# Summing one tile's gathered expert rows by matmuls, and two streams that share six PSUM banks

## The chip, the cores and the metric

One core of a Trainium2 chip runs the kernel. Its engines work in parallel, each through its own queue of instructions in a fixed order: PE (TensorE, matmuls into PSUM), DVE (VectorE), ACT (ScalarE), POOL (GpSimd, which here issues the gathers) and SP (SyncE, which issues all other DMAs). They wait for one another by semaphores. PSUM has eight banks of 128 x 512 fp32. The metric is device microseconds of one execution.

## The reference

One layer of a decoder for 1024 prompt tokens and 8 sample tokens, with d = 1024. The trunk is a combined projection `h @ w_in`, three mixers (dilated attention, gMLP, a linear recurrence) and `w_out`. Behind it comes PEER: each token picks, per head, 16 of 16384 single-neuron experts, 8 x 16 = 128 in all.

```python
x = x + g1 * (mix @ w_out)
h2 = rmsnorm(x, norm_ffn) * (1 + sc2) + sh2
q = rmsnorm((h2 @ w_q).reshape(n, 8, 2, 128))
s = einsum('nhpe,hpke->nhpk', q, sub_keys)        # top 16 of each half, then top 16 of the pairs
act = gelu(einsum('nd,nkd->nk', h2, u_tab[e]))    # 128 rows of u per token
out = einsum('nk,nkd->nd', softmax_gate * act, v_tab[e])   # and 128 rows of v
x = x + g2 * out
```

## The kernel before

The prompt is eight tiles of 128 tokens (0 to 7); tile `NT` = 8 holds the sample tokens. The program has two halves.

The trunk is written group by group (`GROUPS`): `project` (stream Z) makes q, k, v and the mixers B and C of a group's tiles from five blocks of `w_in`; `mix_and_route` (stream R) does attention, `w_out`, the query product with `wq` and the top-16 of the keys; `select` finishes the choice of experts. Each stream takes its PSUM banks from tags of its own: Z two for products (`za`) and one for the rest (`zs`), R two and two, and the gate table of the dense tiles one (`g`), eight in all. `sample_attention` stands behind group 1.

PEER is computed in two ways. Tiles 1, 3, 4 and 5 (`DENSE`) go through all 16384 experts by matmuls (`dense`): 128 chunks of u and v are loaded, split into two fp32r parts, multiplied into `psS`, gated (`a`<-`a`,`gc`) and multiplied into `psK` and `psO`; it starts when the trunk's PSUM and SBUF pools are closed (`fctx.close()`), with `xr` loads from DRAM. Tiles 0, 2, 6 and 7 (`GATHER`) and the sample go through gathered rows (`experts`): for each of the 128 choices k, one indirect DMA of POOL fetches into a `grow` buffer (five of them) the row of choice k for each of the 128 tokens, a token on each partition. A u row is reduced against x by DVE into `dot`; a v row is scaled by DVE and added to `acc` (L933). Each gather moves 128 x 4 KB, 0.524 MB.

The order on each engine is made by a scheduler from the order of the program text: what is written earlier goes first when it is ready. In the text the gathered tiles come last, but their gathers need only POOL, DVE and DMA, so they are taken up as soon as a tile's experts are chosen.

Of the kernel before, what the change touches and what calls it, by code (L numbers as in the profile page):

```python
# [10 lines left out]
F32 = mybir.dt.float32  # L11
F32R = mybir.dt.float32r
BF = mybir.dt.bfloat16
I32 = mybir.dt.int32
U32 = mybir.dt.uint32
AF = mybir.ActivationFunctionType
ALU = mybir.AluOpType
# [4 lines left out]
D = 1024  # L22
NT = 8
GATHER = (0, 2, 6, 7)
DENSE = (1, 3, 4, 5)
PROJECT = ((0, 1, NT), (), (2, 3), (4, 5), (6, 7))
GROUPS = ((0,), (1,), (2, 3, NT), (4, 5), (6, 7))
ND = len(DENSE)
GRP = 4
TB = 16  # L30
OHB = 4
BANKS = dict(za=2, zs=1, ra=2, rs=2, g=1)
GST = 8
LK = 2
SJ = 4
RES = 4
RAW = 6
# [9 lines left out]
P = 128  # L47
# [13 lines left out]
def kernel(ctx: ExitStack, tc: tile.TileContext, I, O):  # L61
    nc = tc.nc
    V, A, G, T, S = nc.vector, nc.scalar, nc.gpsimd, nc.tensor, nc.sync

    dpool = ctx.enter_context(tc.tile_pool(name="dpool", bufs=1, space=DRAM))
    gat = ctx.enter_context(tc.tile_pool(name="gat", bufs=2))
    se = ctx.enter_context(tc.tile_pool(name="se", bufs=1))
    fctx = ExitStack()
    mm = fctx.enter_context(tc.tile_pool(name="mm", bufs=1, space=PSUM))
# [4 lines left out]
    class Stream:  # L74
# [3 lines left out]
            self.key, self.rows = key, rows  # L78

        def ps(self, name="ps", kind="s"):  # L80
            return mm.tile([P, 512], F32, tag="p" + self.key + kind, name=name, bufs=BANKS[self.key + kind])

        def load_w(self, src):
            ws = []
# [16 lines left out]
    R = Stream("r", 4)  # L101

    class Early:

        n = 0
# [18 lines left out]
    ident = fc.tile([P, P], F32, name="ident")  # L124
# [641 lines left out]
            y = rstd(R, qss[t], P, 16, 1.0 / P)  # L766
            V.tensor_tensor(tv[t][0], tv[t][0], y[:, :, None].to_broadcast([P, 16, 16]), op=ALU.mult)

    tr = {}

    def select(t):
        if t == NT:

            tv[t] = (se.tile([P, 16, 16], F32, tag="tkv", name="tkv", bufs=3), se.tile([P, 16, 16], U32, tag="tki", name="tki", bufs=3))
            v1, x1 = (q[:, 0, :] for q in tv[t])
            sr = R.a2("sr")[:, :P]
            S.dma_start(sr, s_d.rearrange("b (s k) -> (b s) k", k=P))
            top16(sr, P, v1, x1, "tkw", P)
            S.dma_start(sv_d, v1)
            S.dma_start(sx_d, x1)  # L780
            v, x = (q[:64, 2:4, :] for q in tv[t])
            S.dma_start(v, sv_d.rearrange("(q two) k -> q two k", two=2))
            S.dma_start(x, sx_d.rearrange("(q two) k -> q two k", two=2))
            r, nh = 64, 1
        else:
            r, nh = P, 8
            v, x = tv[t]
        tv.pop(t)
        i1, i2, gt = (se.tile([P, 8, 16], F32, tag=nm, name=nm, bufs=1)[:r, :nh] for nm in ("d_i1", "d_i2", "d_g"))
        yield from select_experts(v, x, r, nh, i1, i2, gt)  # L790
        if t in h2_d:
            e = se.tile([P, 8, 16], I32, tag="d_q4", name="d_e", bufs=1)[:r, :nh]
            V.scalar_tensor_tensor(e, i1, float(P), i2, op0=ALU.mult, op1=ALU.add)
            for d, src in ((e_d[t], e), (w_d[t], gt)):
                S.dma_start(dram_ap(d, 0, [[16 * nh, r], [1, 16 * nh]]), src.rearrange("p h k -> p (h k)"))
            return
        ps = R.ps("psi")
        tr[t] = fr.tile([P, 3, P], F32, tag="tr", name="tr", bufs=2)
        for q, src in enumerate((i1, i2, gt)):
            T.transpose(ps[:, q * P:(q + 1) * P], src.rearrange("p h k -> p (h k)"), ident)  # L800
        A.copy(tr[t], ps[:, :3 * P].rearrange("p (q n) -> p q n", q=3))

    def gate_ps(name):
        return mm.tile([P, 512], F32, tag="pg", name=name, bufs=BANKS["g"])

    def gate_table(t):

# [106 lines left out]
    def gather_rows(tab, idx):  # L914
        rt = grow("grow")
        G.indirect_dma_start(out=rt, out_offset=None, in_=tab, in_offset=bass.IndirectOffsetOnAxis(ap=idx, axis=0))  # L916
        return rt

    def experts(x, eidx, gate, n):

        w = gat.tile([P, n], F32, tag=f"dot{n}", name="dot", bufs=1)
        for k in range(n):
            rt = gather_rows(I["peer_u"], eidx[:, k:k + 1])
            V.scalar_tensor_tensor(rt, rt, 1.0, x, op0=ALU.mult, op1=ALU.mult, accum_out=w[:, k:k + 1])  # L924
        A.activation(w, w, AF.Gelu_apprx_tanh)
        V.tensor_tensor(w, w, gate, op=ALU.mult)
        acc = gat.tile([P, D], F32, tag="gx", name="acc", bufs=1)
        for k in range(n):
            rt = gather_rows(I["peer_v"], eidx[:, k:k + 1])
            if k == 0:  # L930
                V.tensor_scalar(acc, rt, w[:, 0:1], None, op0=ALU.mult)
            else:
                V.scalar_tensor_tensor(acc, rt, w[:, k:k + 1], acc, op0=ALU.mult, op1=ALU.add)  # L933
        return acc

    def finish(t, peer, alloc):
        g2 = gate_row("g2", t, alloc)
# [13 lines left out]
    def peer_prompt(t):  # L951
        e, w, x = routed(t, [P, P], lambda d: d)
        S.dma_start(x, h2_d[t])
        acc = experts(x, e, w, P)
        finish(t, acc, grow)

    def peer_sample():
# [124 lines left out]
    def now(gen):  # L1082
        for _ in gen:
            pass
# [20 lines left out]
    for t in GROUPS[-1]:  # L1105
        if t in DENSE:
            now(select(t))
            now(gate_table(t))
    fctx.close()
    dense()  # L1110
    for t in GROUPS[-1]:
        if t not in DENSE:
            now(select(t))
    for t in GATHER:
        peer_prompt(t)
    peer_sample()

def _t5_bucket(dist):
# [85 lines left out]
```

## Time and profile before

| | us |
|---|---|
| median of three runs (lowest, highest) | 3285.99 (3276.42, 3286.62) |
| the profiled execution | 3281.25 |
| its span, from the first to the last instruction | 3279.5 |
| busy: PE, DVE, ACT, POOL | 2791.1, 2537.5, 1224.6, 1409.8 |

967.86 MB are moved, 295 GB/s over the span; 545.33 MB of them by POOL's queue. The chain of work that ended last is spread over PE (26% of the span), DMA (22%), the time to issue (21%), POOL (16%) and DVE (10%), so no engine bounds the whole, and the halves are to be read apart. PE's time for an fp32 matmul is written in two records, so 704 products of `psz` stand as 1408.

### The profile page before, as it was taken

To read this page: it belongs to the slowest core of one execution; us is meant where nothing else is said; L and a number is where in the kernel's file an instruction comes from. 1 tells how busy PE (TensorE), PEld (TensorE's weight loads), DVE (VectorE), ACT (ScalarE), POOL (GpSimd) and SP (SyncE) were. 2 spreads that over 40 slices of the span, in tenths; PEclk is the share of its full clock that TensorE was granted. 3 is DMA by queue.
4 is the path that set the end of the run, shared out by engine and by line. 5 is a ranking of instruction groups with operands and counts; after the bars stand their busy time and mean duration, and the time that the engine had idled before them with its cause. 6 is when DMAs were issued, how large, how long until landed. Compare 5 with 4: busy or idle time off the path is not lost.

```text
span 3279.5 us, 36013 instructions
## 1 busy us (share of the span) xinstructions
PE 2791.1 (85%) x11152; PEld 1883.0 (57%) x11152; DVE 2537.5 (77%) x5342; ACT 1224.6 (37%) x2725; POOL 1409.8 (43%) x1046
## 2 busy tenths in 40 slices
PE   6889788789888899777598999888989999889895
PEld 2334334544355445545287777777777777678774
DVE  1434776778877798777999898788888978888986
ACT  3443434755366545656342222221322222222220
POOL 0000323454223431334226655566556556666663
PEclk8889987889999999878799999999999999999997
DMA  7567888897867985788869998899999989999997
GB/s 250 178 210 255 323 270 262 263 352 258 300 211 268 339 279 186 259 281 280 297 235 332 335 342 325 324 326 350 337 330 342 334 308 343 342 344 344 323 337 230
DMA packets 347343, 967.86 MB, mean 295 GB/s; under 512 B 36335, under 2 KB 120870, under 8 KB 345102
## 3 DMA queue, kind: packets, MB, share of 16 engines
q0 software_dynamic: 149760, 545.33, 47.0%
q1 hardware_dynamic: 197390, 420.23, 36.7%
q8 instruction: 88, 1.44, 0.2%
q14 instruction: 105, 0.86, 0.1%
HBM read 909.28 MB, written 60.88 MB: 296 GB/s over the span
## 4 chain that ended last, share of the span: by engine, by line
PE 26%; DMA 22%; issue 21%; POOL 16%; DVE 10%; ACT 4%; SPq 0%; POOLq 0%; DVEq 0%; ACTq 0%
POOL grow L916 16%; PE psz L249 10%; DMA grow<-in_peer_v,ge 8%; DMA g_d<-st 3%; PE psG L823 3%; DMA grow<-in_peer_u,ge 3%; DMA w<-in_wq 2%; DVE acc L933 2%; PE psO L1038 2%; PE pst L174 2%; PE pso L637 2%; PE lg L620 1%; PE psa L206 1%; PE psS L1022 1%; DVE grow L924 1%
## 5 line engine op out<-in xcount | busy, mean ns | idle before, releaser
L916 POOL DMA_INDIRECT grow<-in_peer_u,ge x520 | 698.6, 1343 | 1189.6 <-DVE grow L924 526.1
L916 POOL DMA_INDIRECT grow<-in_peer_v,ge x520 | 710.6, 1366 | 658.5 <-DVE acc L933 365.9
L249 PE MATMUL psz<-w,hT 128*128 128x512 f32 x1408 | 699.2, 629 | 66.8 <-DMA w<-in_wq 33.8
L933 DVE SCALAR_TENSOR_TENSOR acc<-grow,dot,acc 128x1024 f32<-128x1024 f32 x515 | 660.0, 1282 | 117.8 <-DMA grow<-in_peer_v,ge 111.3
L924 DVE SCALAR_TENSOR_TENSOR grow<-grow,gx 128x1024 f32<-128x1024 f32 x520 | 626.1, 1220 | 137.9 <-DMA grow<-in_peer_u,ge 114.0
L249 PEld LDWEIGHTS psz<-w,hT 128*128 128x128 f32 x1408 | 258.5, 201 | 324.9 <-issue 225.4
L1038 PE MATMUL psO<-vh,ah 128*128 128x512 f32 x512 | 225.8, 441 | 138.9 <-DVE acc L1047 138.5
L991 ACT CAST vh<-v 128x1024 fp32r<-128x1024 f32 x128 | 125.2, 1047 | 494.2 <-PE psO L1038 492.3
L823 PEld LDWEIGHTS psG<-o,oh 128*128 128x128 f32 x1024 | 163.9, 221 | 169.3 <-ACT st L825 106.2
L823 PE MATMUL psG<-o,oh 128*128 128x128 f32 x1024 | 197.2, 325 | 69.6 <-ACT st L825 64.0
L991 ACT CAST ah<-a 128x512 fp32r<-128x512 f32 x128 | 79.6, 622 | 435.6 <-DVE a L1027 435.6
L815 DVE TENSOR_TENSOR oh<-iof,tr 128x1024 f32<-128x1024 f32 x128 | 156.4, 1224 | 105.5 <-PE psG L823 104.2
L1038 PE MATMUL psO<-vl,ah 128*128 128x512 f32 x512 | 219.5, 429 | 0.0
L991 ACT CAST uh<-u 128x1024 fp32r<-128x1024 f32 x128 | 134.9, 1054 | 224.5 <-PE psS L1022 224.4
L1038 PE MATMUL psO<-vh,al 128*128 128x512 f32 x512 | 217.9, 426 | 0.0
L1038 PEld LDWEIGHTS psO<-vh,ah 128*128 128x128 f32 x512 | 109.2, 213 | 176.5 <-DVE acc L1047 151.9
L822 ACT ACTIVATE o<-oh,tr 128x128 f32<-128x128 f32 x512 | 185.2, 400 | 55.2 <-PE psG L823 47.9
L1038 PE MATMUL psK<-vh,ah 128*128 128x512 f32 x512 | 201.0, 393 | 4.2 <-ACT ah L991 4.2
L1038 PE MATMUL psK<-vh,al 128*128 128x512 f32 x512 | 200.7, 392 | 0.3 <-DVE al L992 0.3
L1038 PE MATMUL psK<-vl,ah 128*128 128x512 f32 x512 | 200.5, 392 | 0.0
L992 DVE TENSOR_TENSOR ul<-u,uh 128x1024 fp32r<-128x1024 f32 x128 | 156.2, 1220 | 2.8 <-ACT uh L991 2.7
L992 DVE TENSOR_TENSOR vl<-v,vh 128x1024 fp32r<-128x1024 f32 x128 | 150.7, 1220 | 1.3 <-ACT vh L991 1.0
(372 smaller groups left out, 5029.1 us busy)
## 6 DMA issues: line engine op xcount, KB each, us to landing
u<-in_peer_uT SPq DMA_DIRECT2D x128, 512.0 KB
v<-in_peer_v SPq DMA_DIRECT2D x128, 512.0 KB
w<-in_w_in SPq DMA_DIRECT2D x80, 512.0 KB
w<-in_wq SPq DMA_DIRECT2D x80, 512.0 KB
g_d<-st SPq DMA_DIRECT2D x64, 512.0 KB
gc<-g_d SPq DMA_DIRECT2D x16, 2048.0 KB
w<-in_w_ada SPq DMA_DIRECT2D x48, 512.0 KB
w<-in_w_out SPq DMA_DIRECT2D x40, 512.0 KB
```

The source lines that it names most:

```text
L174: T.transpose(pv[:, c, :r], src[:, (c0 + c) * P:(c0 + c + 1) * P], ident[:r, :r])
L249: T.matmul(ps, xT[:, c, :], w(c), start=(c == 0), stop=(c == 7))
L637: T.matmul(po[64 * hh:64 * hh + 64, :P], vt[:, c, 64 * hh:64 * hh + 64], pT[c // 4][:, c % 4, :], start=(c == 0), stop=(c == t))
L815: V.tensor_tensor(oh, iof[:, None, None, :].to_broadcast([P, 2, OHB, P]), tt[:, 0:2, b * TB + n0:b * TB + n0 + OHB, None].to_broadcast([P, ...
L822: A.activation(o1, oh[:, 0, n0 % OHB + q, :], AF.Copy, scale=tt[:, 2, n:n + 1])
L823: T.matmul(ps[:, q * P:(q + 1) * P], oh[:, 1, n0 % OHB + q, :], o1, start=True, stop=True)
L916: G.indirect_dma_start(out=rt, out_offset=None, in_=tab, in_offset=bass.IndirectOffsetOnAxis(ap=idx, axis=0))
L924: V.scalar_tensor_tensor(rt, rt, 1.0, x, op0=ALU.mult, op1=ALU.mult, accum_out=w[:, k:k + 1])
L933: V.scalar_tensor_tensor(acc, rt, w[:, k:k + 1], acc, op0=ALU.mult, op1=ALU.add)
L991: A.copy(hi, x)
L992: eng.tensor_tensor(lo, x, hi, op=ALU.subtract)
L1038: T.matmul(ps, aa[x][:, t * P:(t + 1) * P], vv[y][:, hf * 512:(hf + 1) * 512], start=(k == 0 and (first or o not in keep)), stop=(k == 3 * ...
```

## The change

Tile 0's v rows are gathered by token: for a token, its 128 chosen rows, one on each partition. The indices for that are `eT`, the transpose of the tile's choices, made in `select`. The sum over the 128 choices is then a contraction over partitions, one matmul per half row: its stationary operand is a block `wz` of 32 columns that is zero but for the column of the token, which holds the token's 128 weights from `wT`, so the products of 32 tokens add up in the 32 partitions of their column group. Two PSUM banks (`pacc`) hold the sum of the tile. They are two of the eight; the other six become the tags `a` and `s` of three banks each, for both streams and the gate table. `wz` takes a buffer of R's `a2`. Tile 0's PEER is written in front of `fctx.close()`. `LK`, the buffers of the lookup, goes from 2 to 1.

```diff
--- before.py
+++ after.py
@@ -22,6 +22,7 @@
 D = 1024
 NT = 8
 GATHER = (0, 2, 6, 7)
+ROWS_PE = (0,)
 DENSE = (1, 3, 4, 5)
 PROJECT = ((0, 1, NT), (), (2, 3), (4, 5), (6, 7))
 GROUPS = ((0,), (1,), (2, 3, NT), (4, 5), (6, 7))
@@ -29,9 +30,9 @@
 GRP = 4
 TB = 16
 OHB = 4
-BANKS = dict(za=2, zs=1, ra=2, rs=2, g=1)
+BANKS = dict(a=3, s=3)
 GST = 8
-LK = 2
+LK = 1
 SJ = 4
 RES = 4
 RAW = 6
@@ -78,7 +79,7 @@
             self.key, self.rows = key, rows
 
         def ps(self, name="ps", kind="s"):
-            return mm.tile([P, 512], F32, tag="p" + self.key + kind, name=name, bufs=BANKS[self.key + kind])
+            return mm.tile([P, 512], F32, tag="p" + kind, name=name, bufs=BANKS[kind])
 
         def load_w(self, src):
             ws = []
@@ -766,7 +767,7 @@
             y = rstd(R, qss[t], P, 16, 1.0 / P)
             V.tensor_tensor(tv[t][0], tv[t][0], y[:, :, None].to_broadcast([P, 16, 16]), op=ALU.mult)
 
-    tr = {}
+    tr, eT = {}, {}
 
     def select(t):
         if t == NT:
@@ -791,6 +792,13 @@
         if t in h2_d:
             e = se.tile([P, 8, 16], I32, tag="d_q4", name="d_e", bufs=1)[:r, :nh]
             V.scalar_tensor_tensor(e, i1, float(P), i2, op0=ALU.mult, op1=ALU.add)
+            if t in ROWS_PE:
+                ef = se.tile([P, 8, 16], F32, tag="d_t", name="d_ef", bufs=1)
+                V.scalar_tensor_tensor(ef, i1, float(P), i2, op0=ALU.mult, op1=ALU.add)
+                ps = R.ps("pse")
+                T.transpose(ps[:, :P], ef.rearrange("p h k -> p (h k)"), ident)
+                eT[t] = gat.tile([P, P], I32, tag="eT", name="eT", bufs=1)
+                V.tensor_copy(eT[t], ps[:, :P])
             for d, src in ((e_d[t], e), (w_d[t], gt)):
                 S.dma_start(dram_ap(d, 0, [[16 * nh, r], [1, 16 * nh]]), src.rearrange("p h k -> p (h k)"))
             return
@@ -801,7 +809,7 @@
         A.copy(tr[t], ps[:, :3 * P].rearrange("p (q n) -> p q n", q=3))
 
     def gate_ps(name):
-        return mm.tile([P, 512], F32, tag="pg", name=name, bufs=BANKS["g"])
+        return R.ps(name, "a")
 
     def gate_table(t):
 
@@ -916,7 +924,7 @@
         G.indirect_dma_start(out=rt, out_offset=None, in_=tab, in_offset=bass.IndirectOffsetOnAxis(ap=idx, axis=0))
         return rt
 
-    def experts(x, eidx, gate, n):
+    def weights(x, eidx, gate, n):
 
         w = gat.tile([P, n], F32, tag=f"dot{n}", name="dot", bufs=1)
         for k in range(n):
@@ -924,6 +932,11 @@
             V.scalar_tensor_tensor(rt, rt, 1.0, x, op0=ALU.mult, op1=ALU.mult, accum_out=w[:, k:k + 1])
         A.activation(w, w, AF.Gelu_apprx_tanh)
         V.tensor_tensor(w, w, gate, op=ALU.mult)
+        return w
+
+    def experts(x, eidx, gate, n):
+
+        w = weights(x, eidx, gate, n)
         acc = gat.tile([P, D], F32, tag="gx", name="acc", bufs=1)
         for k in range(n):
             rt = gather_rows(I["peer_v"], eidx[:, k:k + 1])
@@ -933,6 +946,32 @@
                 V.scalar_tensor_tensor(acc, rt, w[:, k:k + 1], acc, op0=ALU.mult, op1=ALU.add)
         return acc
 
+    def experts_by_rows(t, x, eidx, gate):
+
+
+        w = weights(x, eidx, gate, P)
+        ps = R.ps("pswT")
+        T.transpose(ps[:, :P], w, ident)
+        wT = gat.tile([P, P], F32, tag="wT", name="wT", bufs=1)
+        A.copy(wT, ps[:, :P])
+        acc = [mm.tile([P, 512], F32, tag=f"pacc{hf}", name="pacc", bufs=1) for hf in range(2)]
+        for m in range(32):
+            if m % 4 == 0:
+                wz = R.a2("wz").rearrange("p (m j c) -> p m j c", m=4, j=4)
+                V.memset(wz, 0.0)
+                for i in range(4):
+                    V.tensor_copy(wz[:, i, :, m + i], wT.rearrange("p (j m) -> p j m", j=4)[:, :, m + i])
+            for j0 in (0, 2):
+                rows = [(j, gather_rows(I["peer_v"], eT[t][:, 32 * j + m:32 * j + m + 1])) for j in (j0, j0 + 1)]
+                for hf in range(2):
+                    for j, row in rows:
+                        T.matmul(acc[hf][32 * j:32 * j + 32, :], wz[:, m % 4, j, :], row[:, hf * 512:(hf + 1) * 512],
+                                 start=(m == 0), stop=(m == 31))
+        out = gat.tile([P, D], F32, tag="gx", name="acc", bufs=1)
+        for hf in range(2):
+            A.copy(out[:, hf * 512:(hf + 1) * 512], acc[hf])
+        return out
+
     def finish(t, peer, alloc):
         g2 = gate_row("g2", t, alloc)
         x1 = alloc("x1f")
@@ -951,7 +990,7 @@
     def peer_prompt(t):
         e, w, x = routed(t, [P, P], lambda d: d)
         S.dma_start(x, h2_d[t])
-        acc = experts(x, e, w, P)
+        acc = experts_by_rows(t, x, e, w) if t in ROWS_PE else experts(x, e, w, P)
         finish(t, acc, grow)
 
     def peer_sample():
@@ -1106,13 +1145,16 @@
         if t in DENSE:
             now(select(t))
             now(gate_table(t))
+    for t in ROWS_PE:
+        peer_prompt(t)
     fctx.close()
     dense()
     for t in GROUPS[-1]:
         if t not in DENSE:
             now(select(t))
     for t in GATHER:
-        peer_prompt(t)
+        if t not in ROWS_PE:
+            peer_prompt(t)
     peer_sample()
 
 def _t5_bucket(dist):
```

PE around the end of the trunk. `pss` is the trunk's last product, `psS` the dense half's first. Before:

```order
L249 MATMUL psz<-w,hT 128x512 x5
L174 MATMUL pst<-ident,q 128x128 x4
L753 MATMUL pss<-keysT,q2T 128x128 x4
L1022 MATMUL psS<-x0h,uh 128x512
L1022 MATMUL psS<-x0l,uh 128x512
```

and now:

```order
L250 MATMUL psz<-w,hT 128x512 x5
L175 MATMUL pst<-ident,q 128x128 x4
L754 MATMUL pss<-keysT,q2T 128x128 x4
L954 MATMUL pswT<-ident,dot 128x128
L968 MATMUL pacc<-grow,wz 32x512 x256
L1061 MATMUL psS<-x0h,uh 128x512
L1061 MATMUL psS<-x0l,uh 128x512
```

All 256 matmuls on tile 0's v rows, and the transpose of their weights, have come to stand in one run between the two halves.

PE in the trunk, where group 1's attention (`lg_1963`, `pso_1883`, tile 1) is followed by group 2; `hT_2612` before and `hT_2618` now are tile 2's normalised input, `psv` is the sample attention. Before:

```order
L174 MATMUL pst_2702<-ident_75,z_2697 128x128 x4
L249 MATMUL psz_2820<-w_2812,hT_2612 128x512 x2
L637 MATMUL pso_1883<-pT_1896,vt_1881 64x128 x2
L249 MATMUL psz_2820<-w_2814,hT_2612 128x512
L620 MATMUL lg_1963<-kT_1957,qT_733 128x256
L174 MATMUL pst_1907<-ident_75,pr_1884 128x128 x2
L249 MATMUL psz_2820<-w_2814,hT_2612 128x512
L637 MATMUL pso_1883<-pT_1906,vt_1881 64x128 x2
L174 MATMUL pst_1936<-ident_75,pr_1923 128x128 x2
```

and now, where tile 2's projection begins:

```order
L898 MATMUL psv_2554<-vc_2597,pz_2534 64x512
L898 MATMUL psv_2554<-vc_2600,pz_2544 64x512
L908 MATMUL psv_2609<-om_2607,bm_2605 8x512
L175 MATMUL pst_2634<-ident_75,mix_2619 128x128 x4
L175 MATMUL pst_2643<-ident_75,mix_2619 128x128 x4
L250 MATMUL psz_2694<-w_2686,hT_2618 128x512
```

Before, tile 2's projection lies between the steps of tile 1's attention; now it begins behind the last product of the sample attention, with nothing of an earlier group left on PE. The projections of groups 3 and 4 move in the same way.

DVE at the end of the program, where `acc`<-`grow` adds a v row of tile 7, `L1027` (now `L1066`) gates the products of a dense chunk, and `acc`<-`acc`,`grw` begins the tile's last step. Before:

```order
L933 SCALAR_TENSOR_TENSOR acc<-grow,dot,acc 128x1024 x2
L1027 TENSOR_TENSOR a<-a,gc 128x512
L933 SCALAR_TENSOR_TENSOR acc<-grow,dot,acc 128x1024
L992 TENSOR_TENSOR al<-a,ah 128x512
L933 SCALAR_TENSOR_TENSOR acc<-grow,dot,acc 128x1024
L940 TENSOR_TENSOR acc<-acc,grw 128x1024
L1027 TENSOR_TENSOR a<-a,gc 128x512
L941 TENSOR_TENSOR acc<-acc,x1f 128x1024
```

and now, from the dense half's last sums on:

```order
L1105 TENSOR_TENSOR tmp<-grw,acc_11980 128x512
L946 SCALAR_TENSOR_TENSOR acc<-grow,dot,acc 128x1024
L1106 TENSOR_TENSOR x1f<-x1f,tmp 128x1024
L946 SCALAR_TENSOR_TENSOR acc<-grow,dot,acc 128x1024 x70
L979 TENSOR_TENSOR acc<-acc,grw 128x1024
L980 TENSOR_TENSOR acc<-acc,x1f 128x1024
L932 SCALAR_TENSOR_TENSOR grow,dot<-grow,gx 128x1024 x8
```

Tile 7's last rows have moved from between the dense products to behind them. Counted in the order of DVE, 357 gathers are consumed ahead of the first dense gating product before and 128 now (the 128 v rows of tile 0 are consumed on PE); ahead of the last one, 1024 before and 815 now; behind it, besides the sample's 16, none and 81.

## Rows read from the trace of the kernel before

**Rows 1.** Windows: length, busy us of each engine, clock, DMA share, GB/s

```profile
core 0: us, PE busy (x) PEld busy (x) DVE busy (x) ACT busy (x) POOL busy (x), PEclk, DMA share, GB/s
0.00:1608.00 1608.00, 1327.93 (x5008) 691.17 (x5008) 1107.39 (x3426) 804.09 (x2186) 470.10 (x366) 0.89 0.78 266
64.00:192.00 128.00, 113.00 (x384) 45.84 (x383) 55.05 (x173) 54.01 (x117) 0.00 (x0) 0.91 0.56 192
745.00:1608.00 863.00, 726.47 (x2917) 408.07 (x2917) 692.47 (x2083) 471.39 (x1323) 304.01 (x232) 0.90 0.78 268
1640.00:1700.00 60.00, 59.63 (x263) 49.10 (x262) 60.00 (x171) 31.22 (x37) 7.41 (x7) 1.00 0.61 198
1700.00:3190.00 1490.00, 1351.39 (x5673) 1101.53 (x5673) 1276.13 (x1522) 368.55 (x474) 897.55 (x648) 0.94 0.92 335
```

**Rows 2.** Timeline of PE at the trunk's end: start, us, instruction, idle before

```profile
1600.04 4.46 PE L249 MATMUL psz<-w,hT 128*128 128x512 f32 x10
...
1606.75 1.16 PE L753 MATMUL pss<-keysT,q2T 128*128 128x128 f32 x8 [0.92 <-ACT q2T L747]
1635.32 0.76 PE L1022 MATMUL psS<-x0h,uh 128*128 128x512 f32 x1 [27.41 <-ACT uh L991]
```

**Rows 3.** The gathered rows' tile: duration ns min/median/max, first and last start

```profile
L916 POOL DMA_INDIRECT grow<-in_peer_u,ge x520: 932/1332/5442, 350.7 to 3239.7; - x174
...
L916 POOL DMA_INDIRECT grow<-in_peer_v,ge x520: 932/1320/4994, 744.9 to 3257.6; - x174
...
DMA to landing us min/median/max: 4.0/6.7/14.1
```

**Rows 4.** Groups by line from 745 to 1608: busy us, mean ns, idle before

```profile
L916 POOL DMA_INDIRECT grow<-in_peer_v,ge x128 | 169.7, 1326 | 305.3 <-DVE acc L933 114.4 <-DVE tkv L391 40.2 <-DVE sv L391 31.8
L933 DVE SCALAR_TENSOR_TENSOR acc<-grow,dot,acc 128x1024 f32<-128x1024 f32 x127 | 162.2, 1277 | 14.0 <-DMA grow<-in_peer_v,ge 13.3
...
L924 DVE SCALAR_TENSOR_TENSOR grow<-grow,gx 128x1024 f32<-128x1024 f32 x104 | 125.4, 1216 | 5.4 <-DMA grow<-in_peer_u,ge 5.3
...
L760 ACT COPY s<-pss 128x512 f32<-128x512 f32 x23 | 13.4, 582 | 25.0 <-PE pss L753 25.0
...
L401 ACT CAST lk<-d_m 128x1024 bf16<-128x1024 f32 (+1 forms) x9 | 8.7, 966 | 2.9 <-DVE d_i L406 2.9
```

**Rows 5.** Waits of PE from 0 to 1608: us in total, times, longest

```profile
PE psG L823 <- ACT st L825: 64.0, 38, 8.4
PE psz L249 <- DMA w<-in_wq: 33.8, 13, 7.4
```

**Rows 6.** The PSUM tile of the sample attention, and PE idle before

```profile
L890 PE MATMUL psv<-vc,pz x32: 590/643/1116, 474.2 to 520.5; 128*64 128x512 f32 x16, 96*64 96x512 f32 x16
...
  DMA vc<-in_cache_v: 44.5, 17
```

**Rows 7.** Timeline of SP's queue at the start of the dense half

```profile
1615.44 6.01 SPq L998 DMA_DIRECT2D xr<-xT_d  x8
```

**Rows 8.** Timeline of POOL, the closest run of gathers

```profile
3183.58 1.01 POOL L916 DMA_INDIRECT grow<-in_peer_v,ge  x1 [0.30 <-issue]
...
3198.59 1.72 POOL L916 DMA_INDIRECT grow<-in_peer_v,ge  x1 [0.30 <-issue]
```

**Rows 9.** Timeline of DVE at tile 7's last v row

```profile
3214.51 1.28 DVE L933 SCALAR_TENSOR_TENSOR acc<-grow,dot,acc 128x1024 f32<-128x1024 f32 x1
```

**Rows 10.** Timeline of SP's queue at the end

```profile
3218.81 0.34 SPq L942 DMA_DIRECT2D out_xp<-acc  x1
...
3276.80 0.34 SPq L973 DMA_DIRECT2D out_xs<-fin  x1
```

**Rows 11.** Timeline of PE and window: eight matmuls in four column groups

```profile
116.50 3.64 PE L253 MATMUL psz<-w,hT 128*32 128x512 f32 x16 [0.48 <-DVE hss L348]
...
116.00:120.40 4.40, 3.92 (x18) 0.88 (x18) 3.70 (x14) 1.66 (x6) 0.00 (x0) 0.53 0.03 14
```

## The prediction

> **What bounds the kernel now.** I read the slices and the windows first, then who waits for whom, then the queues. The program has two halves. In the trunk (to 1608 us) PE is busy 1328 of 1608 us at a mean granted clock of 0.89 while the DMA engines are 78% busy; in the dense half PE has 0.94, DMA a share of 0.92 and 335 GB/s [rows 1]. The reader is to see that the trunk leaves bandwidth over and the dense half leaves none. GpSimd's queue of row gathers is what uses the spare bandwidth: 360 of its 1040 gathers are issued before 1608 (366 POOL instructions, 6 of them set-up), and 648 in the next 1490 us, which is 2.30 us each [rows 1]. So the end is set by three things: when PE finishes the trunk, how many gathers are still to do then, and at what pace the dense half lets them through. The trunk's last matmul ends at 1607.9 and the dense half's first starts at 1635.3 [rows 2].
>
> **What the change moves.** The queue keeps its order (u of tile 0, v of tile 0, u of tile 2, ...) and its bytes. In the kernel before, tile 0's v rows are consumed by VectorE among trunk work: u rows start at 350.7, v rows at 744.9 [rows 3], and between 745 and 1608 lie all 128 v gathers with 127 accumulations of 1277 ns, and 104 u rows of tile 2 [rows 4]. In the order of instructions 357 gathers are consumed before the first dense product. In the changed kernel the 256 matmuls that consume tile 0's v rows stand on PE behind the last trunk matmul and ahead of the first dense one, because their PSUM tile `pswT` comes last in the shared tag; PE takes its queue in order. The weights are ready far earlier, but only the five `grow` buffers can be filled ahead. So the queue stands still from the end of tile 0's u rows until the trunk is over; only 128 gathers are consumed in the trunk, 128 more in a stretch of their own, and 784 are left.
>
> **(a) The trunk.** It loses the load of some 232 gathers in its second half, and VectorE loses 127 x 1.277 + 104 x 1.216 = 289 us there [rows 4]. PE gains little from that: it waits 64.0 us for `psG` (one bank before, three shared now) and 33.8 us for `wq` weights [rows 5], of which I count the first whole and 21 us of the second (the part behind 745): -85 us at best. Against it stands the lost overlap. With the two streams' banks in one tag, taken in program order, the projections of tiles 2 to 7 no longer lie inside the attention and routing of the group before: 6 tiles x 5 blocks x 8 = 240 matmuls. Ten records of such matmuls take 4.46 us [rows 2], two records a matmul, 0.89 us each: 214 us if nothing shrinks in return. The sample attention, whose 32 records cost PE 44.5 us of waits for `vc` [rows 6], now stands ahead of tile 2's projection instead of beside it. But a projection by itself keeps PE as busy (113 of 128 us, 88%) as the second half is now (726 of 863 us, 84%) [rows 1], so most of the 214 us was work that PE has to do at some time anyway, not filled holes. Bounds -85 and +214; I take +20, nearest to the windows, where the busy share hardly differs. LK = 1 leaves one lookup buffer: at worst VectorE waits for each ScalarE copy into it, 0.97 us [rows 4] x 34 = 33 us; VectorE's freed time covers that, and without the cover it is part of the upper bound.
>
> **(b) From the last trunk matmul to the first dense one: 27.4 us before [rows 2].** Now: 7.5 us of VectorE's last routing before the weight blocks are built (in the kernel before, the `xr` loads start 7.5 us behind the last matmul) [rows 2, 7]; 123 rows beyond the five that are waiting; two copies out of PSUM of 582 ns [rows 4]; and again 19.9 us from the `xr` loads to the first product [rows 2, 7], since these loads stand behind `finish` in SP's queue. The pace of a row: the closest run of issues in the trace is 9 steps in 15.0 us, 1.67 us [rows 8]. The five buffers give (6.7 us median landing [rows 3] + about 2.5 us until PE has done the pair of rows) / 5 = 1.84 us, an estimate from that row. From below: 0.524 MB at the dense half's 335 GB/s is 1.56 us; from above that half's pace, 2.30 us [rows 1]. I take 1.85: 228 us. In all 7.5 + 228 + 1.2 + 19.9 = 257 us, +230 (from +193 to +285). VectorE's routing of tiles 6 and 7 now hides in here. 163 us of VectorE accumulations go, but they lay off the path that ends the trunk.
> The Trainium skill, DMA: Bandwidth & Descriptors (Anatomy of one DMA — SWDGE (gpsimd) path), fits such a transfer as 2.0 us plus its bytes over 436 GB/s, so 1.2 us each once they overlap. By that the 123 rows would be 148 us and the sum 80 us less; the closest issues of this trace stay slower than that, and I go by them.
>
> **(c) The dense half.** Its interleave on VectorE is as dense as before, 20 to 27 gathers to four chunks; 687 gathers are consumed from its first to its last product where 667 were, 20 x 2.30 = +46. Before, its first 60 us took only 7 gathers with PE full [rows 1], for VectorE was routing tiles 6 and 7; the routing leaves, the gathers come sooner. I take +30, between 0 and +46.
>
> **(d) Behind the dense half.** Before, tile 7's last v row is added at 3214.5 [rows 9], with the last dense products. Now 81 of its v rows are still to come behind the last dense gating product (11 of them between the final sums, then 70 in one run). With nobody else loading I take 1.67 us [rows 8]: +135 (1.56 to 2.30: +126 to +186). What follows tile 7 (its result stored from 3218.8, then the sample's rows, the last store at 3276.8) [rows 10] stays as it is.
>
> **Sum.** 20 + 230 + 30 + 135 = +415 us on the profiled execution's own 3281.25 us (span 3279.5, 1.8 around it): 3696 us. That execution lies 0.14% under the median of 3285.99, less than any bound here.
>
> **Rivals.**
> Relief wins: the trunk, without gathers, ends 85 us earlier, and the bare queue runs at the rate of the dense half alone. -85 + 193 + 0 + 126 = +234: 3515. For it: w waits and `psG` waits are there to be taken [rows 5]. Against: the serial projections.
> Overlap lost whole: the holes that the second stream filled stay open, +214 in (a): 3890. For it: attention alone waits on ACT and VectorE at each step; against: the 88%.
> PE sets the pace of (b): if a row's two matmuls ran one after the other at the lower clock level, they would take 2 x 2 x 0.89 = 3.56 us, (3.56 - 1.85) x 123 = +210: 3906. The clock does fall to 0.53 of full speed in a short stretch with few matmuls behind it, but there 8 matmuls of 32 rows in four column groups took 3.64 us, 0.46 us each [rows 11]: column groups run side by side, and here the pairs alternate two. The Trainium skill, TensorE: Matmul & The Clock Gate (Part 3: Packing small matmuls — row/col tiling), says the same of small outputs put in distinct column groups; by it this rival loses most of its chance.
> Faster: the trunk shrinks by more than (b), (c) and (d) cost, 395 us. It would decide if the last trunk matmul ended before 1608 - 395 - 10 = 1203. PE alone is busy 1328 us there; at full clock throughout that would be 1328 x 0.89 = 1182 with no wait at all, so +395 - 426 = -31: 3250. For it only that VectorE and DMA are freed.
> The change does not do what it says to the time: bytes are the same and DMA bounds the dense half, so idle bandwidth could be made up elsewhere: 3281. Against: the dense half has no share left, and its gathers grow.
>
> **Chances.** Forecast 0.60 (its own range 3600 to 3790), relief 0.20, overlap lost 0.10, PE's pace 0.05, faster 0.03, no change 0.02. Leaving out the outer parts of the upper cases and the last two, 8 in 10 lie between 3520 and 3830. A difference of 0.3% is what a measurement of this kernel can tell; slower 0.95, within it 0.02, faster 0.03.
>
> **What would show it.** In the changed profile POOL has no gathers from some 750 us to the end of the trunk; a stretch of 200 to 290 us follows with `pacc` matmuls alone on PE and a gather every 1.6 to 2.2 us; the first dense product starts near 1885 us, the trunk's last at about 1630; at the end some 135 us of accumulations with PE idle. I am wrong if `pacc` matmuls stand between trunk matmuls in time, if the trunk ends under 1540 or over 1720, or if the dense half's gathers come faster than one in 2.2 us.

## The result, and where the time went

The changed kernel takes 3748.36 us (median of 4 runs, 3744.51 to 3761.14) against 3281.20 for the kernel before on the same chip: a ratio of 1.1431, 95% interval 1.1393 to 1.1470. It is 14.3% slower; the forecast was 3696, in a range of 3520 to 3830. Its profiled execution has a span of 3742.7 us, 463 more than before.

The windows of the changed kernel (columns as in [rows 1]) are the trunk, the stretch behind it, the middle of the dense half, and the end:

```profile
0.00:1722.00 1722.00, 1350.49 (x5010) 717.52 (x5010) 873.53 (x3109) 777.57 (x2167) 158.34 (x139) 0.87 0.53 178
1722.00:1961.00 239.00, 196.01 (x514) 45.12 (x513) 64.05 (x308) 18.27 (x25) 123.66 (x128) 0.95 0.88 313
2025.00:3500.00 1475.00, 1335.10 (x5646) 1088.53 (x5645) 1267.44 (x1609) 370.80 (x477) 889.07 (x647) 0.95 0.93 339
3570.00:3743.00 173.00, 0.00 (x0) 0.00 (x0) 112.22 (x99) 0.21 (x1) 103.42 (x81) 0.50 0.79 269
```

Against [rows 1]: the trunk has 139 POOL instructions where it had 366, and yet it is 114 us longer, with the DMA engines at 53% where they were at 78%. The dense half is as before (647 gathers in 1475 us; 648 in 1490). Two stretches are new: 239 us in which TensorE does row sums alone, and an end without TensorE, whose window has 81 gathers, 16 of them the sample's.

PE's timeline (start, us, instruction, idle before) at the trunk's end and at the first dense product, which answers to [rows 2]:

```profile
1720.77 1.16 PE L754 MATMUL pss<-keysT,q2T 128*128 128x128 f32 x8 [0.93 <-ACT q2T L748]
1721.77 0.27 PE L954 MATMUL pswT<-ident,dot 128*128 128x128 f32 x1
1728.13 4.33 PE L968 MATMUL pacc<-grow,wz 128*32 128x512 f32 x18 [6.09 <-DVE wz L963]
...
1936.42 1.91 PE L968 MATMUL pacc<-grow,wz 128*32 128x512 f32 x4 [0.33 <-DMA grow<-in_peer_v,eT]
1960.96 0.77 PE L1061 MATMUL psS<-x0h,uh 128*128 128x512 f32 x1 [22.64 <-ACT uh L1030]
```

The turned weights `pswT` are literally the next matmul behind the trunk's last. POOL's timeline shows the price: five gathers fill the buffers, and the sixth waits 1032 us.

```profile
698.58 0.94 POOL L924 DMA_INDIRECT grow<-in_peer_v,eT  x1 [0.30 <-issue]
1731.87 0.94 POOL L924 DMA_INDIRECT grow<-in_peer_v,eT  x1 [1032.35 <-PE pacc L968]
1733.11 0.94 POOL L924 DMA_INDIRECT grow<-in_peer_v,eT  x1 [0.30 <-issue]
```

DVE at the last gating product of the dense half and at tile 7's last v row, then SP's queue at the end; they answer to [rows 9, 10]:

```profile
3541.27 0.68 DVE L1066 TENSOR_TENSOR a<-a,gc 128x512 f32<-128x512 f32 x1
...
3685.83 1.28 DVE L946 SCALAR_TENSOR_TENSOR acc<-grow,dot,acc 128x1024 f32<-128x1024 f32 x1 [2.58 <-DMA grow<-in_peer_v,ge]
```

```profile
3689.66 0.34 SPq L981 DMA_DIRECT2D out_xp<-acc  x1
...
3739.86 0.34 SPq L1012 DMA_DIRECT2D out_xs<-fin  x1
```

Cut at the same events in both traces, the 463 us are:

| part | before | after | difference | forecast |
|---|---|---|---|---|
| (a) trunk, to the end of the last `pss` | 1607.9 | 1721.9 | +114 | +20 |
| (b) to the first dense product | 27.4 | 239.1 | +212 | +230 |
| (c) to the last gating product | 1581.6 | 1580.3 | -1 | +30 |
| (d) to tile 7's last v row | -2.4 | 144.5 | +147 | +135 |
| (e) from there to the end | 65.0 | 56.9 | -8 | 0 |

What in the trunk is late? Four events of each kernel, by PE's records: the first product with v (`pso`) in the attention of tile 1, and of tile 2 (below, the attention's start), and the last key scores of tiles 2 and 3, and of tiles 6 and 7. In the changed kernel they are at 354, 673, 945 and 1722 us; before at 317, 528, 837 and 1608. So 145 us are lost by the attention of tile 2, and 31 of them come back later. Tile 2's first `pso`, before and now:

```profile
527.66 0.47 PE L637 MATMUL pso<-pT,vt 128*64 128x128 f32 x1
...
672.55 0.66 PE L638 MATMUL pso<-pT,vt 128*64 128x128 f32 x2 [10.94 <-DMA vt<-vt_d]
```

Its waits of PE in the trunk (total us, times, longest) beside [rows 5]:

```profile
PE psG L831 <- ACT o L830: 34.7, 70, 2.5
...
PE pse L799 <- DVE d_ef L797: 25.2, 1, 25.2
...
PE psG L831 <- ACT st L833: 19.6, 16, 1.3
...
PE psz L250 <- DMA w<-in_wq: 10.2, 3, 8.0
```

The waits behind the rows' traffic did shrink (`psG` for `st` from 64.0 to 19.6 us, `wq` from 33.8 to 10.2), but a wait of 25.2 us for the copy of the indices is new.

### The profile page after: what moved, and what is told of

The parts are those of the page before. It is cut to its first block, busy times and chain, and to the rows that moved or that the text cites. A ratio compares the mean times of both kernels' runs of the same rounds, so it can differ in the third digit from the quotient of the medians.

```text
span 3742.7 us, 37005 instructions
## 1 busy us (share of the span) xinstructions
PE 3002.0 (80%) x11666; PEld 1948.5 (52%) x11666; DVE 2433.3 (65%) x5256; ACT 1198.5 (32%) x2708; POOL 1344.8 (36%) x1046
## 3 DMA queue, kind: packets, MB, share of 16 engines
q0 software_dynamic: 149760, 545.33, 41.1%
## 4 chain that ended last, share of the span: by engine, by line
PE 28%; issue 21%; DMA 19%; POOL 15%; DVE 10%; ACT 6%; SPq 0%; POOLq 0%; ACTq 0%; DVEq 0%
POOL grow L924 15%; PE psz L250 12%; DMA grow<-in_peer_v,ge 7%; PE psG L831 3%; DMA grow<-in_peer_v,eT 2%; PE pst L175 2%; PE pso L638 2%; ACT o L830 2%; PE pacc L968 2%; DMA grow<-in_peer_u,ge 1%; DVE acc L946 1%; PE psO L1077 1%; PE psa L207 1%; PE lg L621 1%; DMA w<-in_w_in 1%
## 5 line engine op out<-in xcount | busy, mean ns | idle before, releaser
L924 POOL DMA_INDIRECT grow<-in_peer_u,ge x520 | 683.4, 1314 | 944.0 <-DVE grow L932 388.8
L250 PE MATMUL psz<-w,hT 128*128 128x512 f32 x1408 | 660.1, 613 | 42.2 <-DMA w<-in_w_in 21.4
L924 POOL DMA_INDIRECT grow<-in_peer_v,ge x392 | 536.5, 1369 | 311.9 <-DVE acc L946 211.7
L946 DVE SCALAR_TENSOR_TENSOR acc<-grow,dot,acc 128x1024 f32<-128x1024 f32 x388 | 497.7, 1283 | 112.5 <-DMA grow<-in_peer_v,ge 105.5
L924 POOL DMA_INDIRECT grow<-in_peer_v,eT x128 | 124.3, 971 | 1121.1 <-PE pacc L968 1101.4
L1077 PE MATMUL psO<-vh,ah 128*128 128x512 f32 x512 | 224.8, 439 | 144.5 <-DVE acc L1086 141.2
L968 PE MATMUL pacc<-grow,wz 128*32 128x512 f32 x512 | 195.9, 610 | 20.3 <-DMA grow<-in_peer_v,eT 13.7
```

Of the source, the lines that this page charges most:

```text
L250: T.matmul(ps, xT[:, c, :], w(c), start=(c == 0), stop=(c == 7))
L968: T.matmul(acc[hf][32 * j:32 * j + 32, :], wz[:, m % 4, j, :], row[:, hf * 512:(hf + 1) * 512], start=(m == 0), stop=(m == 31))
L1077: T.matmul(ps, aa[x][:, t * P:(t + 1) * P], vv[y][:, hf * 512:(hf + 1) * 512], start=(k == 0 and (first or o not in keep)), stop=(k == 3 * ...
```

## The experiments

Theory at the start: shared tags, whose banks are handed out in program order, make the trunk longer (S); the same order puts tile 0's rows behind the trunk, since `pswT` and `wz` take slots of the stages' rings (the buffers of one tag, used in turn) and are written last (O). Rivals: six banks are too few in any form (B); the row sum's own parts in the trunk cost it (N).

**1. Sharing alone, on the kernel before.**

```
-BANKS = dict(za=2, zs=1, ra=2, rs=2, g=1)
+BANKS = dict(a=3, s=3)          # and tag="p" + kind; the gate tables take R's "a"
```

> The kernel before with one edit: its streams share two tags of three banks each (six banks in all), and all rows stay on VectorE. Theory S (the shared tags, whose banks are handed out in program order, keep the second projection behind stages that it ran beside): the trunk ends 80 to 130 us later than the 1608 us of the kernel before, most of it by the end of the projection of tiles 2 and 3; dense half and tail as before; 3360 to 3410 us in all. Rival N (the 114 us that the trunk lost come from the row sum's own parts in the trunk: the transpose of the indices with its wait of 25.2 us, the gathers' new order, the one lookup buffer): 3270 to 3300 us, no change.

Measured: 3527.0 us, ratio 1.0737 (1.0690 to 1.0784). The trunk ends at 1940 us, +333, far more than either theory had.

```profile
0.00:1940.00 1940.00, 1431.76 (x5006) 765.45 (x5007) 1314.36 (x3620) 785.35 (x2168) 639.13 (x518) 0.82 0.77 263
```

Tile 2's attention starts at 640 us (528 before): that is S, and N falls. But the loss goes on to the end of the trunk, in which now lie 512 gathers, 152 more than before. The dense half has only 528 rows and is 48 us shorter. Against the changed kernel (1722 us, 133 gathers) the question became what a gather costs the trunk.

**2. Six banks with own tags, on the kernel before.**

```
+BANKS = dict(za=1, zs=1, ra=1, rs=2, g=1)
```

> The kernel before with six banks in place of eight, but each stream with tags of its own (two streams' logits and projection tags have one bank where they had two). Theory S (sharing costs, not the number): trunk 0 to 40 us later, 3280 to 3325 us. Rival B (six banks are too few, shared or not): as in the changed kernel, trunk 80 to 130 us later, 3360 to 3410 us.

Measured: 3371.3 us, ratio 1.0268 (1.0250 to 1.0287); trunk 1743 us, tile 2's attention at 542, 403 gathers. The trunk lost a little more than rival B said (+135; 80 to 130), but not where the sharing loses it: the projection is nearly in time (+14), the rest comes behind it. Fewer banks cost, and sharing them costs again.

**3. The row sum's slots out of the trunk's rings, in the changed kernel.**

```
-        ps = R.ps("pswT")
+        ps = mm.tile([P, 512], F32, tag="pacc0", name="pswT", bufs=1)
-                wz = R.a2("wz")...
+                wz = gat.tile([P, D], F32, tag="gx", name="wz", bufs=1)[:, :512]...
```

> The changed kernel with two slots of its row sum taken out of the trunk's rings: the transposed weights go through the bank of the first accumulator, the four zero-padded weight blocks through the buffer that later takes the sum. Theory O (the sum of tile 0 stood behind the trunk only because its slots are handed out in program order, and it is written last): the first of its matmuls moves from 1728 us into the middle of the trunk, the stretch of 239 us between trunk and dense half falls to about 27, the 81 rows behind the dense half are gathered in the trunk again and the 147 us of tail go; the trunk keeps its 114 us: 3748 - 212 - 147 = 3390, with 3360 to 3440. Rival P (the matmuls in order on TensorE then wait for rows inside the trunk at the pace of the gathers, 1.64 us a row, and the trunk takes what the stretch gives back): 3550 to 3620 us. Rival G (gathering queue still stands still between tile 0's last row and the trunk's end because tile 2 is written behind the dense half): the tail keeps some 100 us or more, about 3490.

Measured: 3571.1 us, ratio 1.0866 (1.0828 to 1.0904). Theory O is right on the place: the `pacc` matmuls move to 721 to 1245 us, the stretch falls to 28 us, the dense half ends the kernel with nothing behind it. Its sum is wrong: the trunk takes 1976 us, 254 more, with 508 gathers where there were 133. The time is in rival P's range; PE's matmuls waited only 15 us for rows, though (the 41.1 of the tile count its weight loads too):

```profile
L968 PE MATMUL pacc<-grow,wz x512: 589/592/1063, 721.1 to 1245.1; 128*32 128x512 f32 x171
...
  DMA grow<-in_peer_v,eT: 41.1, 25
...
PE pacc L968 <- DMA grow<-in_peer_v,eT: 14.9, 9, 3.8
...
0.00:1976.00 1976.00, 1515.85 (x5522) 752.25 (x5522) 1164.50 (x3517) 783.94 (x2172) 598.59 (x515) 0.86 0.74 256
```

The row sums themselves now keep PE busy in the trunk: 1516 us where it was 1350. So 165 of the 254 us are PE's busy time, and the gathers are not the whole of it.

**4. Half of the matmuls of the sum.**

```
-                for hf in range(2):     # around the matmuls; both halves are then copied from acc[0]
+                for hf in range(1):
```

> The changed kernel with half of the row sum's matmuls left out: only the first 512 columns of tile 0 are summed, and are copied to both halves; 256 of 512 matmuls go, all gathers stay. Theory D (the stretch behind the trunk goes at the pace of the gathers, 1.64 us a row): it stays at 205 to 215 us and the whole at 3735 to 3760. Rival E (TensorE's matmuls, busy 195.9 of its 210 us, set the pace): it falls to 100 to 130 us, the whole to 3640 to 3670.

Measured: 3742.2 us, ratio 1.1402 (1.1383 to 1.1422). With half of TensorE's work the row stretch falls from 210.2 to 195.9 us (1735.5 to 1931.4), a little under theory D's range and far above E's: gathers and their landing set most of the pace, and TensorE adds 14 us.

```profile
1729.00:1954.00 225.00, 135.49 (x261) 18.06 (x260) 64.19 (x311) 18.11 (x25) 123.42 (x128) 0.90 0.92 332
```

**5. The queue standing still, with all eight banks.** The kernel before; tile 0 is written ahead of the dense half, and its weights take a slot of the stages' ring:

```
+        if late_rows:                   # tile 0 only
+            w2 = R.a2("w2")[:, :n]
+            V.tensor_copy(w2, w)
+            w = w2
```

> The kernel before, eight banks and all rows on VectorE, but tile 0's weights are copied once into a buffer of the stages' ring that is handed out last, so that its rows of v are gathered behind the trunk, as in the changed kernel. No bank, TensorE instruction or lookup is changed. Theory R (a row that is gathered in the trunk costs the trunk time; by the shared-bank kernel with 512 gathers in its trunk of 1940 us and the changed kernel with 133 in 1722, some 0.58 us a row): with 227 gathers fewer the trunk falls from 1608 to about 1475 (1440 to 1520); the stretch of 128 rows adds 210 to 240, the tail about 140: 3480 to 3540 us in all. Rival H (rows in the trunk are hidden, and the shared-bank kernel's trunk is longer by the banks alone): trunk 1590 to 1610, 3600 to 3660.

Measured: 3508.3 us, ratio 1.0692 (1.0651 to 1.0733). Theory R to the number: the trunk ends at 1480.3 us (1475 was expected).

```profile
0.00:1480.00 1480.00, 1282.51 (x5007) 661.54 (x5008) 854.84 (x3104) 799.16 (x2186) 177.08 (x139) 0.92 0.63 207
```

```profile
PE psG L823 <- ACT st L825: 31.8, 29, 4.9
...
PE psz L249 <- DMA w<-in_wq: 13.6, 5, 6.3
```

POOL again waits, 723 us here:

```profile
763.25 0.94 POOL L916 DMA_INDIRECT grow<-in_peer_v,ge  x1 [0.30 <-issue]
1487.29 2.01 POOL L916 DMA_INDIRECT grow<-in_peer_v,ge  x1 [723.10 <-DVE ny L164]
```

So tile 0 written ahead of the dense half and one copy in the wrong ring, with no bank and no TensorE row sum changed, makes about half of the loss: 251 us of stretch and 199.5 us behind the last gating product (62.5 before), for a trunk that is 128 us shorter.

**6. Own tags in the changed kernel.** `BANKS` and tags as in experiment 2.

> The changed kernel with tags of their own for the streams in the same six banks (one each, two for the attention's second). Theory S (shared tags keep the projection of tiles 2 and 3 behind stages): the attention of tile 2 starts at 540 to 570 us in place of 673, the trunk ends near 1743 - 0.58 x 270 = 1586 (1560 to 1630), the rest stays: 3590 to 3650 us. Rival W (the loss to 673 us comes from the row sum's own parts): no change, 3730 to 3760.

Measured: 3607.0 us, ratio 1.0999 (1.0955 to 1.1043); trunk 1589.2 us (1586 was expected), tile 2's attention at 588 us, a little above S's 540 to 570. S holds; the stretch (237 us) and the end stay. Tile 1's attention starts at 380 us, though, 40 later than in experiment 2.

**7. Both edits together.** Experiment 3's slots and experiment 6's tags.

> The changed kernel with both edits: slots of its own for the row sum and own tags in six banks. Theory R with S: trunk near 1743 + 0.58 x 105 = 1800 (1770 to 1840), then 28 and a dense half of some 1560 with its few last us: 3370 to 3440 us, still slower than the kernel before. Rival P (TensorE's row matmuls hold the trunk by waiting for their rows): trunk 1860 to 1930, 3460 to 3530.

Measured: 3491.9 us, ratio 1.0639 (1.0598 to 1.0680). The time falls in P's range and for another reason: the trunk ends at 1696 us, before either theory, but holds only 270 gathers, and 81 rows are left behind the dense half. The row sums were now spread over 864 to 1654 us, and the queue stood behind them:

```profile
POOL grow L924 <- PE pacc L968: 566.0, 60, 82.0
```

Against experiment 6 the trunk is 107 us longer with 137 more gathers, but PE is busy 123 us more in it, with row sums (below, experiment 6 and this one):

```profile
0.00:1589.00 1589.00, 1325.38 (x5009) 675.86 (x5010) 869.35 (x3114) 797.32 (x2182) 156.21 (x139) 0.90 0.58 193
...
0.00:1696.00 1696.00, 1448.46 (x5522) 700.81 (x5522) 881.78 (x3151) 791.47 (x2177) 299.92 (x276) 0.90 0.66 224
```

**8. VectorE's work on tile 0's rows cut to an eighth**, on the kernel before: 128 of 1024 columns in the dots and in the sum.

```
+            V.scalar_tensor_tensor(rt[:, :m], rt[:, :m], 1.0, x[:, :m], ...)   # m = 128 for tile 0
```

> The kernel before with VectorE's work on tile 0's 256 rows cut to 128 of 1024 columns (the other columns are left out of the dots and of the sum); all rows are still gathered whole. Some 280 us of VectorE's work in the trunk go. Theory V (a row costs the trunk VectorE's time): the trunk falls by 80 us or more, to under 1530, although some 60 rows of tile 2 move up into it. Theory M (a row costs the trunk by its transfer of 512 KB beside the stages' own loads, or by its wait): the trunk stays at 1600 to 1650.

Measured: 3300.7 us, ratio 1.0048 (1.0021 to 1.0074). VectorE is busy 962 us in the trunk (1107 before), which yet ends at 1655, 5 us above theory M's range, with 431 gathers. At 0.56 us each (experiment 5) the 71 gathers more would give 1648, so the 145 us less of VectorE's work bought nothing. Theory V falls.

```profile
0.00:1655.00 1655.00, 1324.15 (x5008) 691.67 (x5008) 961.94 (x3525) 796.98 (x2184) 473.68 (x437) 0.88 0.80 281
```

**9. Without turning the indices**, in the kernel of experiment 6.

```
-                ps = R.ps("pse")
-                T.transpose(ps[:, :P], ef.rearrange("p h k -> p (h k)"), ident)
```

> The changed kernel with own tags in six banks, and without the turning of tile 0's indices: the second copy as floats, its transpose on TensorE and the copy back are left out, and rows are gathered by the untransposed indices (the sum is that of other rows; count and size of the gathers are the same). In the kernel with own tags, tile 1's attention starts at 380 us, in the six-bank kernel before at 340. Theory T (TensorE stands behind the transpose, which waits 25.2 us for the indices): it starts at 345 to 355, the trunk ends 25 to 40 us earlier, at 1550 to 1565, and the whole at 3565 to 3585. Rival L (the 40 us come from the single lookup buffer): no change, 3595 to 3620.

Measured: 3560.8 us, ratio 1.0895 (1.0848 to 1.0942). Theory T, with the time a little under its 3565: tile 1's attention at 342 us, the trunk's end at 1555.3, 34 us earlier.

**10. One lookup buffer**, on the kernel before: `LK = 1`.

> The kernel before with one lookup buffer in place of two, and nothing else. Rival L: tile 1's attention starts 20 to 40 us later than 317, the whole takes 3300 to 3330 us. Theory T: no change, 3275 to 3295.

Measured: 3305.9 us, ratio 1.0123 (1.0082 to 1.0164). The time is rival L's, the mechanism is not: tile 1's attention starts at 309 us, not later, and the trunk is 18 us shorter, with 335 gathers in place of 360. From the last gating product to the end it is 96.5 us in place of 62.5. Gathers that leave the trunk come back at the end; a buffer moved them.

**11. Own banks for the projections alone**, in the changed kernel.

```
+BANKS = dict(za=1, zs=1, a=2, s=2)
```

> The changed kernel with one bank for each of the projections' two tags, apart from the others; the attention, the routing and the gate tables go on sharing two banks for each of theirs: six in all. Theory Z (what sharing costs is that a projection, written later, gets a bank only after stages written before it): the attention of tile 2 starts at 580 to 610 us in place of 673, the trunk ends at 1580 to 1640, the whole takes 3590 to 3660 us. Rival A (the attention's and the gate tables' turns for a shared bank cost as much): 650 to 680, 1690 to 1730, 3710 to 3760.

Measured: 3676.6 us, ratio 1.1237 (1.1196 to 1.1277), between the two ranges: tile 2's attention starts at 586 us, as Z said, but the `pso` products of tiles 2 and 3 take 159 us (85 in experiment 6, 117 in the changed kernel), and the trunk ends at 1657. The projection's place is 65 us of the sharing; the turns of attention and gate tables are the other 68.

**12. Short rows**: tile 0's gathers cut to 64 KB, on the kernel before.

```
+        G.indirect_dma_start(out=rt[:, :m], ..., in_=tab.rearrange("n (b m) -> (n b) m", m=m), ...)
+            hold = R.a2("hold")[:, :1]      # behind tile 0's sum
```

> The kernel before with tile 0's 256 gathers cut to 128 of 1024 columns (64 KB in place of 512 KB each, the rest left out; its indices then point into the first eighth of the table) and VectorE's work on them cut likewise; tile 0's sum passes once through a buffer of the stages' ring that is handed out last, so that no row of tile 2 is read before the trunk's end. The trunk then holds 256 short gathers and the 5 that fill the buffers. Trunks so far: 133 whole gathers 1480 us, 360 whole ones 1608, 0.56 us a gather, so 261 whole ones would give about 1552. Theory M (a gather costs the trunk by the bytes that it moves beside the stages' own loads): 1480 or less, down to 1410 since tile 0's u rows shrink too. Rival Q (it costs by its place in the queues or by its instructions): 1530 to 1570. The time of the whole is longer by what is left behind the trunk and tells nothing.

Measured: the trunk ends at 1559 us, in rival Q's range (3378.6 us in all, ratio 1.0292, 1.0197 to 1.0387, by two runs). So the bytes of a row are not the whole price either. By this trace, in which some records are missing, VectorE waited 88 us between 340 and 900 us for rows to land:

```profile
DVE grow L924 <- DMA grow<-in_peer_u,ge: 55.3, 45, 2.8
DVE acc L933 <- DMA grow<-in_peer_v,ge: 32.6, 31, 2.1
```

In experiment 5, whose v rows come later, it was 24.2 us in the same stretch. It fits that trunk work stands behind a row in VectorE's queue until the row has landed; that this makes the 79 us was not shown.

## Why the prediction was right, and which step was off

**Right in the mechanism.** The order of instructions said that PE takes tile 0's row sum behind the trunk, that the queue then stands still, and that 784 gathers are left. The trace shows each of them, and experiments 3 and 5 show the cause from both sides: take the slots out of the ring, and stretch and end go; put one copy into the ring of the kernel before, and both come.

**(a) is the mis-sized term: +20 forecast, +114 measured.** By the prediction's own sign (a trunk over 1720) it was wrong here, by 2 us. The step that failed is that the busy shares of two windows decide between its bounds. They hid terms much larger than their sum. The runs separate them in one order, each step between two kernels by its trunk:

| step | trunk, us | difference |
|---|---|---|
| before: eight banks, 360 gathers in the trunk | 1607.9 | |
| rows late, 133 gathers (experiment 5) | 1480.3 | -128 |
| six banks, own tags, one lookup buffer, row sum without the turn (9) | 1555.3 | +75 |
| with the turn of the indices (6) | 1589.2 | +34 |
| attention, routing and gate tables share (11) | 1657.4 | +68 |
| the projections share too (the changed kernel) | 1721.9 | +65 |

The ends of the trunk in experiments 5, 9, 6 and 11:

```profile
1479.19 1.16 PE L753 MATMUL pss<-keysT,q2T 128*128 128x128 f32 x8 [0.92 <-ACT q2T L747]
...
1554.16 1.16 PE L754 MATMUL pss<-keysT,q2T 128*128 128x128 f32 x8 [0.93 <-ACT q2T L748]
...
1588.02 1.16 PE L754 MATMUL pss<-keysT,q2T 128*128 128x128 f32 x8 [0.93 <-ACT q2T L748]
...
1656.25 1.16 PE L754 MATMUL pss<-keysT,q2T 128*128 128x128 f32 x8 [0.93 <-ACT q2T L748]
```

Each is one execution. Experiment 4 changes nothing in the trunk, and its trunk is 7 us longer than the changed kernel's, so a few microseconds say nothing.

The relief was put at 85 us at best, and was 128: the two waits of PE that were counted fell by 52 us (64.0 to 31.8, 33.8 to 13.6), its other idle time by 30, and its busy time by 45 at a mean granted clock of 0.92 in place of 0.89 (experiment 5). The losses were put at 214 at most, and were 242. In the 75 us, fewer banks and the single lookup buffer aren't separated; on the kernel before, the buffer alone made the trunk no longer (experiment 10), and the same six banks made it 135 us longer with 43 more gathers (experiment 2), so a step's size depends on the kernel that it is taken in. The turn of the indices was priced at nothing: it is a single transpose, but PE, in order, waited 25.2 us ahead of it.

**(b) +230 forecast, +212 measured.** The parts: 6.2 us to the first row matmul (7.5 forecast), 210.2 for the rows (228), 22.7 to the first product (21.1). By the prediction's 123 rows that is 1.71 us a row where 1.85 was taken (1.64 over all 128), close to the 1.67 of the closest issues [rows 8]. That the gathers and not TensorE set it, the rival at 3906, is settled by experiment 4. By the fit in the Trainium skill, DMA: Bandwidth & Descriptors (Anatomy of one DMA — SWDGE (gpsimd) path), the bytes of each would take 1.2 us, an estimate that no row stretch here reaches: 1.53 us is the least. The Trainium skill, TensorE: Matmul & The Clock Gate (Part 3: Packing small matmuls — row/col tiling), has small outputs in distinct column groups run side by side; the trace agrees: the four records that end the stretch, the two matmuls of one late row, take 1.91 us one after another, and the 18 that begin it, with rows waiting for all four column groups, 4.33 us, where that pace would make 8.6.

**(c) +30 forecast, -1 measured.** The step "20 more rows at 2.30 us" is wrong: 2.30 us is how often a row fits in, not what it costs. The dense half took 1534 us with 528 rows (experiment 1), 1568 with 639 (2), 1582 with 667 (before) and 1580 with 687: some 0.3 us a row. That is rough, for with 687 rows it took from 1565 us (experiment 9) to 1583 (11).

**(d) +135 forecast, +147 measured**: 81 rows as forecast, at 1.78 us in place of 1.67 (144.5 / 81). **(e)** 8 us less than before; not looked into.

Rivals: "relief wins" had a relief (85 for 128) and nothing against it. "Overlap lost whole" had no relief, and a loss near in size (214 for 242) by luck: it put all of it to the projections' lost overlap, whose place is 65 us, and 133 with all of the sharing. The sample attention's waits of 44.5 us [rows 6], which the prediction put to PE, count its weight loads too; its matmuls waited 17.6 us before and 33.1 now. The forecast's 52 us too few are 94 in (a) and 12 in (d), less 18, 31 and 8 in (b), (c) and (e), and 3 us from the other ends, which come from medians and spans. That the sum came so near is in part luck: errors of +106 and -57 us offset each other.

**What stays open.** What a gather costs the trunk: 0.56 us from experiment 5 (128 / 227). Between the changed kernel and experiment 3 it looks like 0.68 (254 / 375), but 165 of those 254 us are PE's busy time, and between 6 and 7 PE's added 123 us are more than the trunk's 107; what the gathers cost beside the row sums is not shown. VectorE's work is not it (8), and the row's bytes are not all of it (12). These experiments also move the order of instructions, so the parts can't be priced one by one. No run is faster than the kernel before, and none points to a version that would be: its rows lie where a gather is cheap (0.3 us in the dense half until that is full, some 0.6 in the trunk), and only those behind the dense half cost their full 1.8 us.

## What to carry to other kernels

Where slots of a ring are handed out in program order, one tile that is written last and taken from a busy ring holds back all that depends on it, and whatever queues behind that: look at the slot first, not at the data. A background stream is priced by where it ends up: moving it costs little while another stage still has room, and its full pace once nothing is beside it. And where the two sides of a term are large, bound each side by itself; an equal busy share before and after says little of what was exchanged.

## Not expected

- Of the same gather, 512 KB by a list of 128 rows: 1.64 us each with TensorE's row sums alone (210.2 / 128; 313 GB/s over the whole 239 us), 1.53 with half of them (195.9 / 128; 332 GB/s over 225 us), and 1.78 at the very end.
- With 227 gathers fewer in the trunk, TensorE's mean granted clock rose from 0.89 to 0.92; with 152 more, and shared banks, it fell to 0.82. TensorE was busy 83% of the trunk before, 87% and 74% in these two.
- The sample attention's matmuls waited 33.1 us for `vc` in the changed kernel, 17.6 before, although the DMA engines were less busy over the trunk.
